# Hybrid decoder step on one core: down-weight differences moved from the attention to the input projection, a third slot for down operands, and another order at the block ends

## The chip, the core and the metric

The kernel runs on one core of a Trainium2 chip. The metric is the time of one execution on the device in microseconds (us). The core has five engines that work side by side and wait for each other by semaphores: PE (matrix products), DVE (vector), ACT (scalar functions and copies), POOL (a second, slower vector engine here) and SP, which in this kernel issues almost all DMA transfers. Each engine executes its instructions strictly in the order in which they were written into its queue.

## The reference, cut to what matters

The function is one step of a decoder layer for a prompt of 2048 positions and a sample group of 32 rows (8 sequences of 4 positions, behind caches of earlier keys and values), followed by a final norm. The model width is 1024, the FFN width 2816.

```python
def _layer_prompt(x, ...):
    q, k, v, u, vg = _project(x, norm1_g, w_in)          # RMSNorm, one product with w_in (1024 x 2560)
    ...
    for (w, d), bias_hj in zip(BRANCHES, biases):        # 8 heads, three dilated windows
        o, l = _dilated_prompt(q, k, v, bias_hj, d, w // d + 1)
    ...
    gate = _spatial_gate(vn, sgu_w, sgu_b).reshape(B, S, D_SGU)
    x = x + jnp.concatenate([att, u * gate], axis=-1) @ w_out
    x = x + _swiglu(x, norm2_g, w_gate, w_up, w_down)
    return x, k[:, S - nw:], v[:, S - nw:]

def _swiglu(x, g, w_gate, w_up, w_down):
    h = _rmsnorm(x, g)
    return (jax.nn.silu(h @ w_gate) * (h @ w_up)) @ w_down
```

The sample rows go through the same layer with the cached keys and values in front of their own, and the window of keys and values is copied into the outputs.

## The kernel before

**Precision.** Everything is fp32, but PE multiplies operands in a shorter format. So each operand is split into a high part (an ACT copy into the short format) and a low part (a subtraction, value less high part, on DVE or POOL), and one product is three matmuls: high by high, high by low, low by high. "Splitting" below always means this pair of operations. In the names, `xh` and `xl`, or the two halves of a `hop` tile, are such parts.

**Stages.** The input projection (0 to 565 us of the span) runs over 240 steps of 24 matmuls each. The order of all that goes on beside them is a list: `Plan.at(step, phase, fn, ...)` files a function under a step and a phase, and `Plan.run` calls them in that order, which writes the instructions into the queues. Beside PE's work lie the sample group's scores and values (`pr`, `kv`, `qv`: cached values loaded by SP; POOL products L539; matmuls L600), and the writing of projected rows to memory. From step B0 = 240 the same list holds the attention (565 to 905 us): for each head and branch `band_scores` (PE, L867 and, for the wide-stride branch, L946) writes scores into the banks `ps_s`, `band_bias` (DVE, L873 and L951) adds the bias and frees the bank, ACT takes exponents, POOL masks and prepares operands (`sq`, `e`), PE turns and multiplies with the values.

**The weights of the down projection.** The FFN is multiplied with a scheme of Strassen's kind: seven products in place of eight, of sums and differences of blocks. The down weights `w_down` are 22 row tiles; a pair n of them (n = 0 to 10), each cut into two column halves of 512, gives the blocks b11, b12 (first row tile) and b21, b22 (second). Seven operands of 128 x 512 per n are kept in memory as `dd_d[n, :, 0..6]`: three plain blocks (copied from memory to memory by `down_plain`, in the projection) and the four differences, made in the attention by `down_rows` (load), `down_sums` (L1231 and L1234: two subtractions on POOL, two on DVE per n) and `down_keep` (store). In the attention they are called at steps 3, 8 to 11 and 11 to 14 of every 14.

**Blocks.** Then the 16 row tiles go in three blocks of 6, 6 and 4, the last one with the sample rows. A block opens with its output projection: `open_unit` (first half of the columns; three matmuls L1414 to L1416 for each of 8 operands, `ps_t`) and `second_unit`, norm (`norm2_*`, L1448 to L1518), then the FFN: for each of 22 hidden tiles f, seven products (`product`, L1799 to L1801), and beside them `h_even` and `h_odd`, which form the operands `hop` of the down products for a pair of hidden tiles, and the down products of the pair before (`down_product`, L1676: 9 matmuls each with 6 tiles). A product index is k = 7n + p. Within the FFN time runs in ticks, one per product; at each, `one(u, q)` calls what is due. Down products stand at SLOT = 2, 4, 6, ... 14 of a pair's 14 ticks.

**Down operands.** `load_dw` (SP) brings operand k into one of the two slots of `B.ring`, `split_dw` splits it (ACT L1655; L1656 on DVE in block 0, on POOL in block 1), `down_product` uses it two ticks after the split is written. Block 1 stores all split operands to `ds_d` (`keep_dw`), and block 2 loads them from there, high and low part, without splitting.

**Block ends.** The last pair's down products (k = K to K + 6 with K = 70) are executed in `next_block`, among the first output units of the following block. There `later(n, fn)` files a function n ticks ahead and `tick()` runs what is due. `h_last` forms the last operands; `split_dw` splits; `finals` are the final norms of the old block's tiles, after each of which the tile's accumulator is stored and loaded with the next block's input rows (`load_acc`); `first_end` adds an output unit's result to it. In the last block the sample rows' unit comes first; its normed rows live in `xns`, in the slot of accumulator 5.

## Time and profile before

| | |
|---|---|
| median of 3 runs | 2578.89 us (2577.04 to 2584.58) |
| profiled execution | 2574.83 us |
| its span | 2573.1 us |
| mean granted PE clock over the span | 0.979 |
| transfers, whole span | 567.45 MB, mean 221 GB/s |

In the views that follow, a row of the windows table gives a stretch of the span, its length, and for each engine the busy time with its number of instructions; then PE's granted clock (1 is full speed), the mean busy share of the 16 DMA engines and what they moved. A row of the waits names the waiting engine, its output and line, what it waited for, and then the total, the number of waits and the longest one in us. A row of the timeline has the start, the duration, engine, line and operation, and in brackets the idle time ahead of it and what ended it. A row by tile or line has the number of instructions and the shortest, median and longest in ns, then the start of the first and the last. A row of the costliest groups has busy time, mean ns of one, and the idle time of the engine ahead of them.

### The profile page before, as it was taken

Reading aid. Unit: us, or ns where it says so; the run is one execution under the profiler, and the core shown is the slowest. Engines: PE = TensorE matmul, PEld = TensorE weight load, DVE = VectorE, ACT = ScalarE, POOL = GpSimd, SP = SyncE. Lnnn points to the kernel's source line nnn. Section 1 sums busy time; section 2 is a strip of 40 time slices with the busy share of each in tenths; the row PEclk is TensorE's granted clock in tenths of the full one; section 3 lists DMA queues with packets and bytes.
Section 4 is the critical chain, followed back from the end, with each engine's and each line's share of the span. In section 5 each row is a group of like instructions: output and inputs, shape, how many; then the busy total and the mean of one; then the engine's idle time right before and its main releaser. Section 6 shows DMA issues by size and latency. Waiting matters only on the chain.

```text
span 2573.1 us, 40785 instructions
## 1 busy us (share of the span) xinstructions
PE 2428.4 (94%) x13764; PEld 2083.0 (81%) x13764; DVE 1683.4 (65%) x3254; ACT 1206.2 (47%) x2703; POOL 1388.9 (54%) x1130
## 2 busy tenths in 40 slices
PE   8999999998989898999999989999999987999997
PEld 6877776667777778899999968988988875988886
DVE  4558572216767645777778777677766766677776
ACT  6324343225656646656666446333433335433334
POOL 2116441004877746777676734655655554666664
PEclk9999999998999899999999999999999998999999
DMA  9975766776668563666667543777777754788884
GB/s 288 282 222 165 240 190 217 224 255 214 236 208 259 161 192 123 212 221 202 223 210 229 187 139 140 235 250 247 244 244 240 242 183 144 266 282 283 285 276 161
DMA packets 360132, 567.45 MB, mean 221 GB/s; under 512 B 36247, under 2 KB 168520, under 8 KB 354804
## 3 DMA queue, kind: packets, MB, share of 16 engines
q1 hardware_dynamic: 353076, 552.78, 66.3%
q10 hardware_dynamic: 6848, 12.06, 1.7%
q8 instruction: 110, 1.80, 0.3%
q14 instruction: 98, 0.80, 0.1%
HBM read 428.77 MB, written 214.73 MB: 250 GB/s over the span
## 4 chain that ended last, share of the span: by engine, by line
PE 36%; POOL 13%; issue 11%; DVE 8%; DMA 7%; ACT 5%; SPq 1%; POOLq 0%; DVEq 0%; ACTq 0%
POOL op L1590 5%; PE ps_o L1676 5%; PE ps_m L1799 4%; PE ps_m L1801 4%; PE ps_m L1800 4%; DMA hop<-dd_d 2%; PE ps_m L1676 2%; PE ps_s L867 1%; POOL sq L938 1%; ACT fr L1558 1%; ACT op L1586 1%; PE ps_o L922 1%; DMA ds_d<-hop 1%; DVE acc L1678 1%; PE ps_s L321 1%
## 5 line engine op out<-in xcount | busy, mean ns | idle before, releaser
L1590 POOL TENSOR_TENSOR op<-fr,op 128x512 fp32r<-128x512 f32 x385 | 505.9, 1330 | 252.4 <-ACT op L1586 240.7
L1799 PE MATMUL ps_m<-xh,op 128*128 128x384 f32 (+3 forms) x1904 | 606.7, 319 | 4.1 <-DVE zn L1820 1.7
L1800 PE MATMUL ps_m<-xl,op 128*128 128x384 f32 (+3 forms) x1904 | 604.4, 317 | 0.8 <-DVE xl L141 0.7
L1801 PE MATMUL ps_m<-xh,op 128*128 128x384 f32 (+3 forms) x1904 | 605.0, 318 | 0.0
L1676 PE MATMUL ps_o<-hop 128*128 128x512 f32 x1272 | 345.9, 401 | 30.6 <-POOL hop L1656 11.8
L1799 PEld LDWEIGHTS ps_m<-xh,op 128*128 128x128 f32 x1904 | 359.9, 189 | 17.8 <-PE ps_m L1801 2.7
L1800 PEld LDWEIGHTS ps_m<-xl,op 128*128 128x128 f32 x1904 | 359.8, 189 | 10.1 <-issue 0.9
L1801 PEld LDWEIGHTS ps_m<-xh,op 128*128 128x128 f32 x1904 | 359.6, 189 | 0.0
L1678 DVE TENSOR_TENSOR acc<-acc,ps_o 128x512 f32<-128x512 f32 x448 | 294.4, 682 | 34.3 <-PE ps_o L1676 30.8
L1676 PEld LDWEIGHTS ps_o<-hop 128*128 128x128 f32 x1272 | 230.0, 188 | 90.1 <-POOL hop L1656 21.7
L1586 ACT ACTIVATE op<-fr 128x512 fp32r<-128x512 f32 x396 | 236.1, 620 | 0.4 <-issue 0.2
L321 PE MATMUL ps_s<-wh,xh 128*128 128x512 f32 x480 | 198.4, 413 | 6.5 <-ACT xh L138 5.9
L322 PE MATMUL ps_s<-wl,xh 128*128 128x512 f32 x480 | 190.1, 396 | 0.0
L323 PE MATMUL ps_s<-wh,xl 128*128 128x512 f32 x480 | 189.9, 396 | 0.0
L1839 ACT ACTIVATE ps_t<-zn 128x384 f32<-128x384 f32 (+1 forms) x126 | 58.3, 463 | 266.7 <-DVE zn L1822 137.1
L1656 POOL TENSOR_TENSOR hop<-hop 128x512 fp32r<-128x512 f32 x71 | 91.8, 1293 | 168.9 <-ACT hop L1655 156.3
L1655 ACT ACTIVATE hop<-hop 128x512 fp32r<-128x512 f32 x142 | 88.8, 625 | 178.5 <-DMA hop<-dd_d 131.3
L539 POOL TENSOR_TENSOR pr<-kv,qb 96x512 f32<-96x512 f32 x32 | 45.7, 1428 | 176.7 <-DMA kv<-in_cache_k_dram 96.0
L321 PEld LDWEIGHTS ps_s<-wh,xh 128*128 128x128 f32 x480 | 91.7, 191 | 49.3 <-issue 23.7
L1590 POOL TENSOR_TENSOR op<-pair,op 128x512 fp32r<-128x512 f32 x63 | 92.6, 1470 | 61.2 <-ACT op L1586 58.1
L1656 DVE TENSOR_TENSOR hop<-hop 128x512 fp32r<-128x512 f32 x71 | 74.3, 1047 | 76.7 <-ACT hop L1655 71.7
L1676 PE MATMUL ps_m<-hop 128*128 128x512 f32 x426 | 122.2, 395 | 0.0
(525 smaller groups left out, 5118.2 us busy)
## 6 DMA issues: line engine op xcount, KB each, us to landing
fr<-ab_d SPq DMA_DIRECT2D x308, 256.0 KB
hop<-dd_d SPq DMA_DIRECT2D x142, 256.0 KB
ds_d<-hop SPq DMA_DIRECT2D x140, 256.0 KB
hop<-ds_d SPq DMA_DIRECT2D x140, 256.0 KB
out_ks_dram<-in_cache_k_dram SPq DMA_DIRECT2D x56, 512.0 KB
out_vs_dram<-in_cache_v_dram SPq DMA_DIRECT2D x56, 512.0 KB
ab_d<-fr SPq DMA_DIRECT2D x88, 256.0 KB
qk_d<-pair SPq DMA_DIRECT2D x64, 256.0 KB
```

Source lines behind the costliest of these rows:

```text
L321: pe.matmul(o[j], xh[:, k, :], wh, start=(k == 0), stop=False)
L322: pe.matmul(o[j], xh[:, k, :], wl, start=False, stop=False)
L323: pe.matmul(o[j], xl[:, k, :], wh, start=False, stop=(k == KD - 1))
L1586: act.activation(ops[f, j][0], ab[f][j], AF.Copy)
L1590: (pool if f or j in POOL_LOW else dve).tensor_sub(lo_, ab[f][j], hi.bitcast(F32))
L1655: act.activation(hi, lo_.bitcast(F32), AF.Copy)
L1656: (pool if B.b0 else dve).tensor_sub(lo_, lo_.bitcast(F32), hi.bitcast(F32))
L1676: pe.matmul(ps, l_, r_, start=(new and y == 0), stop=(y == 2), skip_group_check=True)
L1678: dve.tensor_add(x[:, cs], x[:, cs], ps)
L1799: pe.matmul(out, wh[:, ks], xh[:, :, k], start=(k == 0), stop=False)
L1800: pe.matmul(out, wh[:, ks], xl[:, :, k], start=False, stop=False)
L1801: pe.matmul(out, wl[:, ks], xh[:, :, k], start=False, stop=(k == 3))
```

## The change

Three parts.

1. The four differences of each n are made in the input projection, at steps 124 + 9n to 124 + 9n + 14, all on POOL, each in place in one of seven rotating tiles of 128 x 512 (`tw`): b11 becomes b12 - b11, b12 becomes b22 - b12, then b22 becomes b22 less the new b11, and b21 becomes b21 less that: the same four operands as before, in other places of `dd_d` (PLACE follows). `down_plain` moves out of the projection: three n in the attention, eight in block 0's FFN. SP has 44 loads and 44 stores of 256 KB in place of 22 loads of 512 KB and 44 stores of 256 KB.
2. The ring of down operands has three slots. Operand k + 3 is loaded right behind product k, and split three ticks ahead of its product. Block 2 loads the same unsplit operands as the others and splits them, every third on DVE and the others on POOL; `ds_d`, `keep_dw` and their 280 transfers are gone. In block 2 `h_even` runs on DVE instead of POOL.
3. `next_block` has another order of down products and output units, of the splits, of `h_last` (three parts instead of four), and of the ticks of the halves, finals and ends. The concatenated operands of the first two tiles are loaded in the last ticks of the FFN. Before the last block the finals run in the order 4, 5, 0, 1, 2, 3 instead of 4, 0, 1, 2, 3, 5.

```diff
-    def down_plain(n, j):
-        f, half = 2 * n + (j > 0), int(j == 3)
-        sync.dma_start(dd_d[n, :, j], A["w_down"][f * P:(f + 1) * P, half * 512:(half + 1) * 512])
+    dn = {}
+    def down_rows(n, *js):
+        for j in js:
+            dn[n, j] = w_ = sp.tile([P, 512], F32, name="tw", tag="tw", bufs=7)
+            r0 = (2 * n + j // 2) * P
+            sync.dma_start(w_, A["w_down"][r0:r0 + P, j % 2 * 512:(j % 2 + 1) * 512])
+    def down_sums(n, part):
+        b11, b12, b21, b22 = (dn.get((n, j)) for j in range(4))
+        for x, y, z in (((b11, b12, b11), (b12, b22, b12)), ((b22, b22, b11),), ((b21, b21, b22),))[part]:
+            pool.tensor_sub(x, y, z)
+    def down_keep(n, *js):
+        for j in js:
+            sync.dma_start(dd_d[n, :, 1 + j], dn.pop((n, j)))
+    def down_plain(n):
+        f = 2 * n
+        sync.dma_start(dd_d[n, :, 0], A["w_down"][f * P:(f + 1) * P, 0:512])
+        sync.dma_start(dd_d[n, :, 5:7], A["w_down"][(f + 1) * P:(f + 2) * P, :].rearrange("p (a c) -> p a c", a=2))
...
     for n in range(NF // 2):
-        for y, j in enumerate((0, 2, 3)):
-            at(134 + 6 * n + 2 * y, "store", down_plain, n, j)
+        s0 = 124 + 9 * n
+        at(s0, "misc", down_rows, n, 0, 1, 3)
+        at(s0 + 6, "misc", down_rows, n, 2)
+        for part in range(3):
+            at(s0 + 9 + part, "out", down_sums, n, part)
+        at(s0 + 13, "store", down_keep, n, 0, 1)
+        at(s0 + 14, "store", down_keep, n, 3, 2)
...
-    def down_rows(n):
-        for z in range(2):
-            dn[n, z] = w_ = ap_.tile([P, 2, DA], F32, name="tw", tag="tw", bufs=4)
-            f = 2 * n + z
-            sync.dma_start(w_, A["w_down"][f * P:(f + 1) * P, :].rearrange("p (a c) -> p a c", a=2))
-    def down_sums(n, j, eng):
-        (b11, b12), (b21, b22) = ((dn[n, z][:, 0], dn[n, z][:, 1]) for z in range(2))
-        if j == 1:
-            eng.tensor_sub(b12, b12, b11)
-            return
-        dn[n, "t", j] = t_ = ap_.tile([P, DA], F32, name="tu", tag="tu", bufs=6)
-        eng.tensor_sub(t_, *((b22, b12) if j < 4 else (b21, dn[n, "t", 2])))
-    def down_keep(n, j):
-        if j == 1:
-            sync.dma_start(dd_d[n, :, 1], dn.pop((n, 0))[:, 1])
-        else:
-            sync.dma_start(dd_d[n, :, j + 2], dn.pop((n, "t", j)))
-    for n in range(NF // 2):
-        s0 = B0 + 3 + 14 * n
-        at(s0, "misc", down_rows, n)
-        for j, x, eng in ((3, 5, pool), (1, 6, dve), (2, 7, pool), (4, 8, dve)):
-            at(s0 + x, "store", down_sums, n, j, eng)
-        for j, x in ((3, 8), (1, 9), (2, 10), (4, 11)):
-            at(s0 + x, "store", down_keep, n, j)
+    for n in range(3):
+        at(B0 + 40 + 30 * n, "store", down_plain, n)
...
-        B.ring = [(ts[z][:, 1536:], ts[z + 1][:, 1536:]) for z in (0, 2)]
+        x = fl.tile([P, 512], F32R, name="dwx", tag="dwx", bufs=1)
+        B.ring = [(ts[0][:, 1536:], ts[1][:, 1536:]), (ts[2][:, 1536:], ts[3][:, 768:1280]), (ts[3][:, 1280:1792], x)]
...
     def load_dw(B, k, place=None):
         n, p = divmod(k, 7)
-        B.dw[k] = x = place or B.ring[k % 2]
-        if B.last:
-            for z in range(2):
-                sync.dma_start(x[z].bitcast(F32), ds_d[n, p, z])
-        else:
-            sync.dma_start(x[1].bitcast(F32), dd_d[n, :, PLACE[p]])
+        B.dw[k] = x = place or B.ring[k % 3]
+        sync.dma_start(x[1].bitcast(F32), dd_d[n, :, PLACE[p]])
     def split_dw(B, k):
         hi, lo_ = B.dw[k]
         act.activation(hi, lo_.bitcast(F32), AF.Copy)
-        (pool if B.b0 else dve).tensor_sub(lo_, lo_.bitcast(F32), hi.bitcast(F32))
-    def keep_dw(B, k):
-        n, p = divmod(k, 7)
-        for z in range(2):
-            sync.dma_start(ds_d[n, p, z], B.dw[k][z].bitcast(F32))
+        (dve if B.b0 == 0 or B.last and k % 3 == 0 else pool).tensor_sub(lo_, lo_.bitcast(F32), hi.bitcast(F32))
...
-        eng = pool if B.last or B.b0 == 0 else dve
+        eng = pool if B.b0 == 0 else dve
...
-        B.banks = {i: y for y, i in enumerate(order)}
+        B.banks = {i: (2, 3, 4, 0, 1, 5)[y] for y, i in enumerate(order)}
         B.place()
         tiles = [i for i in order if B.rows[i] == P]
         skip = n - len(tiles)
         for j, i in enumerate(tiles):
-            if j < 3:
-                load_cat(B, i, 0, KD)
-            else:
-                later(2 * j - 5, load_cat, B, i, 0, KD)
-            later((3, 7, 11, 13, 15, 17)[j + skip], split_cat, B, i, dve if j < 2 else pool)
+            if j > 1:
+                later(2 * j - 4, load_cat, B, i, 0, KD)
+            if j:
+                later((0, 1, 5, 8, 10, 12)[j], split_cat, B, i, dve if j % 2 else pool)
...
         for y, fn in enumerate(finals):
-            later(13 + y, fn)
+            later(14 + y, fn)
         for y, i in enumerate(order):
-            later(8 + 2 * n + 2 * y, first_end, B, i)
+            later((19 if B.last else 20) + 2 * y, first_end, B, i)
         for y in range(4):
-            later(13 + 2 * y, half1_split, B, 2 * y, 2 * y + 1)
-            later(15 + 2 * y, sources, B, 0, *((2 * y, 2 * y + 1) if y < 3 else (6,)))
-        K, opens = 7 * (NF // 2 - 1), list(order)
+            later(14 + 2 * y, half1_split, B, 2 * y, 2 * y + 1)
+            later(16 + 2 * y, sources, B, 0, *((2 * y, 2 * y + 1) if y < 3 else (6,)))
+        K = 7 * (NF // 2 - 1)
         def downs(*ks):
             for k in ks:
                 down_product(prev, k)
                 tick()
+        def opens(*ys):
+            for y in ys:
+                open_unit(B, order[y])
+        downs(K - 1)
+        split_dw(prev, K + 1)
         h_last(prev, prev.u, 0)
-        downs(K - 1)
+        downs(K)
+        h_last(prev, prev.u, 1)
         split_dw(prev, K + 2)
-        h_last(prev, prev.u, 1)
-        downs(K + 4)
+        opens(0)
         h_last(prev, prev.u, 2)
         split_dw(prev, K + 3)
-        downs(K)
-        h_last(prev, prev.u, 3)
+        split_dw(prev, K + 4)
+        opens(1)
         split_dw(prev, K + 5)
-        open_unit(B, opens.pop(0))
+        downs(K + 1, K + 2, K + 3)
         split_dw(prev, K + 6)
-        downs(K + 1, K + 2)
-        open_unit(B, opens.pop(0))
-        downs(K + 3, K + 5, K + 6)
-        for i in opens:
-            open_unit(B, i)
+        opens(2)
+        downs(K + 4, K + 5, K + 6)
+        opens(*range(3, n))
         first_operands(B)
...
-                    for y, p in {3: ((0, 0), (1, 1)), 4: ((2, 2), (3, 3)), 5: ((4, 5), (5, 6))}.get(q, ()):
-                        c0 = (y - 4) * 28 * 64 + 512 if y > 3 and nb.last else y * 28 * 64
-                        load_dw(B, 7 * (f // 2) + p, tuple(x[:, c0:c0 + 512] for x in pool_["X"]))
-                    for p in {5: (0,), 6: (4, 1)}.get(q, ()):
-                        split_dw(B, 7 * (f // 2) + p)
+                    for y in {3: (0, 1), 4: (2, 3), 5: (4,)}.get(q, ()):
+                        c0 = 768 if y == 4 and nb.last else y * 28 * 64
+                        load_dw(B, 7 * (f // 2) + 2 + y, tuple(x[:, c0:c0 + 512] for x in pool_["X"]))
+                    if q == 5:
+                        load_cat(nb, 0, 0, KD)
+                        split_dw(B, 7 * (f // 2))
+                    if q == 6:
+                        load_cat(nb, 1, 0, KD)
+                        split_cat(nb, 0, pool)
...
-                    if x == t_ and p == 5 and n + 2 == NF // 2 and nb:
-                        down_product(B, k)
-                        load_dw(B, k + 6, B.ring[k % 2])
-                        continue
                     if n < 0 or n + 1 == NF // 2:
                         continue
-                    if x == t_ - 2 and not B.last:
+                    if x == t_ - 3:
                         split_dw(B, k)
-                    if x == t_ - 1 and nb and nb.last:
-                        keep_dw(B, k)
                     if x == t_:
                         down_product(B, k)
-                    t_ = 14 * ((k - 2) // 7 + 1) + SLOT[(k - 2) % 7] if k > 1 else 9 + k
-                    if x == t_:
+                        if k + 3 < 7 * (NF // 2 - 1) + (2 if nb else 0):
+                            load_dw(B, k + 3)
+                    if k < 3 and x == 8 + k:
                         load_dw(B, k)
+            if bi == 0 and f % 2 == 0 and f < NF - 6 and q == 2:
+                down_plain(f // 2 + 3)
...
-            last = ([4] if nb.last else []) + [i for i in rows if not (nb.last and i == 4)]
+            last = [4, 5, 0, 1, 2, 3] if nb.last else rows
```

How the order changes on the engines, at three places. First DVE in the attention, at the sixth of the eleven n. `ps_s` are score banks, `b` the bias, `e` the biased scores and `st` their sums; `tw` and `tu` are the down weights and their differences. Before:

```order
L905 COPY pt<-ps_o_6974 128x2x128
L873 ISA e,st<-ps_s,b 128x640
L873 ISA st 128x1
L1231 TENSOR_TENSOR tw<-tw 128x512
L905 COPY pt<-ps_t_7009 128x2x128
L873 ISA e,st<-ps_s,b 128x640
L873 ISA st 128x1
L873 ISA e,st<-ps_s,b 128x128
L873 ISA st 128x1
L965 TENSOR_REDUCE st<-e_6960 128x4
L1234 TENSOR_TENSOR tu<-tw,tu 128x512
```

The same place of the changed kernel (L929 is L905 of before, L897 is L873, L989 is L965):

```order
L929 COPY pt<-ps_o_7041 128x2x128
L897 ISA e,st<-ps_s,b 128x640
L897 ISA st 128x1
L929 COPY pt<-ps_t_7074 128x2x128
L897 ISA e,st<-ps_s,b 128x640
L897 ISA st 128x1
L897 ISA e,st<-ps_s,b 128x128
L897 ISA st 128x1
L989 TENSOR_REDUCE st<-e_7027 128x4
```

The two subtractions are gone from between the score operations, and nothing else has moved; the same holds for POOL in the attention.

Second, SP in the projection of the changed kernel, around the end of one n and the start of the next. `raw` are columns of `w_in`, `qv`, `pr` and `kv` cached values of the sample, `qk_d` projected rows on their way to memory.

```order
L633 DMA dd_d<-tw 128x512 x2
L524 DMA qv<-in_cache_v_dram 96x512
L633 DMA dd_d<-tw 128x512 x2
L612 DMA cs_d<-zn 4x512
L623 DMA tw<-in_w_down_dram 128x512
L524 DMA qv<-in_cache_v_dram 96x512
L524 DMA pr<-in_cache_v_dram 96x512
L520 DMA kv<-in_cache_v_dram 96x512
L357 DMA qk_d<-pair 128x4x128 x2
L527 DMA pr<-in_cache_v_dram 128x512
L520 DMA kv<-in_cache_v_dram 96x512
L623 DMA tw<-in_w_down_dram 128x512 x3
```

In the kernel before, the queue there has one copy of a plain block (L619) every two steps and nothing of `tw`. Now the single load (the fourth row tile of the next n) stands directly behind the four stores of this one, and it is the eighth use of the seven tiles.

Third, PE at the end of block 0. L1676 (L1667 after) are the matmuls of down products, with one bank name for each pair of tiles; L1414 to L1416 (L1413 to L1415 after) those of output units. Before, from the last FFN product on:

```order
L1676 MATMUL ps_o_15112<-hop 128x512 x3
L1676 MATMUL ps_o_15117<-hop 128x512 x3
L1676 MATMUL ps_m_15122<-hop 128x512 x3
L1676 MATMUL ps_o_15194<-hop 128x512 x3
L1676 MATMUL ps_o_15199<-hop 128x512 x3
L1676 MATMUL ps_m_15204<-hop 128x512 x3
L1676 MATMUL ps_o_15222<-xh_9302,hop 128x512
L1676 MATMUL ps_o_15222<-xl_9303,hop 128x512
```

Of the changed kernel:

```order
L1667 MATMUL ps_o_15109<-hop 128x512 x3
L1667 MATMUL ps_o_15114<-hop 128x512 x3
L1667 MATMUL ps_m_15119<-hop 128x512 x3
L1667 MATMUL ps_o_15181<-hop 128x512 x3
L1667 MATMUL ps_o_15186<-hop 128x512 x3
L1667 MATMUL ps_m_15191<-hop 128x512 x3
L1413 MATMUL ps_m_15220<-op,xh_9285 128x512
L1414 MATMUL ps_m_15220<-op,xh_9285 128x512
L1415 MATMUL ps_m_15220<-op,xl_9286 128x512
```

The third product, K (K + 4 stood second), is gone from the head, and the first output unit stands there. In all, the order was K - 1, K + 4, K, a unit, K + 1, K + 2, a unit, K + 3, K + 5, K + 6 and the other units; it is K - 1, K, two units, K + 1 to K + 3, a unit, K + 4 to K + 6 and the other units.

More of the change, by code (lines that the diff above doesn't have):

```diff
@@ L122, in hymba_step @@
     dd_d = dram.tile([NF // 2, P, 7, 512], F32, name="dd_d")
-    ds_d = dram.tile([NF // 2, 7, 2, P, 512], F32, name="ds_d")
     ident = consts.tile([P, P], F32, name="ident")
@@ L1454, in norm2_a @@
         else:
-            s1 = fl.tile([P, 4], F32, name="s1", tag="s1", bufs=6)
+            s1 = s1_tile()
             if n != P:
@@ L1765, in h_last @@
             high_of(B, 1, u["s2"], 0, n)
-            for z in (1, 0):
-                high_of(B, 3, a22[z], 0, n, z)
-        elif part == 2:
+        elif part == 1:
             lows_of(B, 1, u["s2"], 0, n)
@@ L2214, in next_block @@
             if front:
-                ahead = (front[0], norm2_t(B, *front, two(ps_m, 0, 1) if (front[0] + B.last) % 2 else None))
+                ahead = (front[0], norm2_t(B, *front, [lambda: ps_m(2), lambda: bank(0)] if front[0] % 2 else two(ps_m, 0, 1)))
             front = i, chain(B, i, ps, ahead)
             if B.last and i == tiles[0]:
-                norm2_c(B, n - 1, B.xns)
+                norm2_c(B, n - 1, B.xns, two(ps_m, 0, 1))
         if B.last:
```

26 lines of the change are left out of this document (13 added, 13 removed).

## The prediction

> **What bounds the kernel now.** First the page's busy times, then the table of windows, cut at the program's stages: the input projection, the attention, and for each token block its opening (last down products, output units, norm) and its FFN. A window's length minus PE's busy time is PE's idle time; PEclk is the granted clock.
>
> ```profile
> PE 2428.4 (94%) x13764; PEld 2083.0 (81%) x13764; DVE 1683.4 (65%) x3254; ACT 1206.2 (47%) x2703; POOL 1388.9 (54%) x1130
> ```
>
> ```profile
> core 0: us, PE busy (x) PEld busy (x) DVE busy (x) ACT busy (x) POOL busy (x), PEclk, DMA share, GB/s
> 300.00:565.00 265.00, 255.78 (x1219) 181.60 (x1220) 98.73 (x191) 82.29 (x136) 51.05 (x38) 0.99 0.69 218
> 565.00:905.00 340.00, 305.12 (x2616) 251.71 (x2614) 230.71 (x549) 207.59 (x528) 237.37 (x241) 0.94 0.68 216
> 905.00:1035.00 130.00, 118.44 (x645) 102.37 (x643) 59.09 (x140) 75.28 (x176) 70.07 (x63) 0.96 0.50 160
> 1035.00:1482.00 447.00, 438.13 (x2263) 404.35 (x2264) 339.89 (x571) 256.71 (x649) 320.89 (x245) 0.99 0.67 213
> 1482.00:1520.00 38.00, 26.99 (x105) 20.12 (x104) 30.18 (x43) 12.48 (x23) 10.43 (x6) 0.91 0.54 157
> 1520.00:1602.00 82.00, 79.41 (x422) 67.93 (x420) 58.79 (x143) 50.41 (x108) 39.75 (x25) 1.00 0.37 126
> 1602.00:2082.00 480.00, 467.69 (x2450) 430.33 (x2449) 338.80 (x558) 185.35 (x384) 289.57 (x222) 1.00 0.75 244
> 2082.00:2110.00 28.00, 21.46 (x91) 15.49 (x90) 18.98 (x31) 9.60 (x19) 17.21 (x13) 1.00 0.62 186
> 2110.00:2197.00 87.00, 70.95 (x336) 57.84 (x335) 53.84 (x136) 47.29 (x103) 34.79 (x23) 0.88 0.37 124
> 2197.00:2520.00 323.00, 318.90 (x2098) 289.81 (x2097) 246.39 (x496) 128.16 (x325) 194.56 (x166) 1.00 0.82 282
> ```
>
> PE is busy 94% of the span, and the change removes no matmul. What it can win is PE's idle time and the time at a lower clock. In the attention (565 to 905) that is 340 - 305.1 = 34.9 us idle, and a clock 6% short over 340 us, some 20 us of work. The two places where one block ends and the next opens idle 11.0 + 2.6 us (1482 to 1602) and 6.5 + 16.1 us (2082 to 2197, clock 0.88). The three FFN stages idle 8.9, 12.3 and 4.1 us. So I read the waits there, the attention's first.
>
> ```profile
> PE ps_s L946 <- DVE st L873: 16.5, 7, 6.3
> PE ps_s L867 <- DVE st L873: 15.1, 13, 4.0
> ...
> POOL tu L1234 <- DMA tw<-in_w_down_dram: 28.1, 2, 23.3
> DVE tw L1231 <- POOL tu L1234: 15.7, 6, 5.1
> ```
>
> 16.5 + 15.1 = 31.6 of the 34.9 us are PE waiting for DVE to free a score bank. DVE itself stood in L1231, a weight difference, for POOL's, 15.7 us; and POOL stood for the down weights' load. The timeline has the chain whole:
>
> ```profile
> 586.33 1.26 POOL L1234 TENSOR_TENSOR tu<-tw 128x512 f32<-128x512 f32 x1 [23.28 <-DMA tw<-in_w_down_dram]
> ...
> 587.62 1.51 DVE L1231 TENSOR_TENSOR tw<-tw 128x512 f32<-128x512 f32 x1 [5.06 <-POOL tu L1234]
> ...
> 590.36 1.94 PE L946 MATMUL ps_s<-sq 128*128 128x128 f32 x8 [6.30 <-DVE st L873]
> 626.44 1.94 PE L946 MATMUL ps_s<-sq 128*128 128x128 f32 x8 [2.45 <-DVE st L873]
> 768.55 1.08 PE L946 MATMUL ps_s<-sq 128*128 128x128 f32 x8 [2.67 <-DVE st L873]
> ```
>
> The load lands, POOL subtracts, DVE's in-place subtraction goes 1.3 us later, and the scores behind it in DVE's queue free PE's bank after 6.30 us. Eight such matmuls take 1.08 us at full clock and 1.94 us behind two of these gaps.
>
> **The change, part by part.** I sum against the profiled execution, 2574.83 us (span 2573.1), which is 4.06 us under the median of the runs, 2578.89.
>
> *1a. The differences leave the attention.* All 44 subtractions go, 22 on POOL and 22 on DVE, with every wait on them. PE's order there is the same, so its tempo tells the worth. One score step (L951) is the beat:
>
> ```profile
> L951 DVE TENSOR_TENSOR e<-ps_s,b x24: 675/680/683, 617.2 to 850.2; 128x512 f32<-128x512 f32 x24
> ...
> L951 DVE TENSOR_TENSOR e<-ps_s,b x9: 676/680/683, 651.0 to 724.5; 128x512 f32<-128x512 f32 x9
> ```
>
> The whole run of 24 has 23 beats in 233.0 us, 10.13 us each. The nine between 651.0 and 724.5, where only small waits fall, have 8 beats in 73.5 us, 9.19 us each. 23 x 0.94 = 21.6 us. Ahead of the first beat lies the 6.30 us gap, and the matmuls behind it lost 0.86 us (1.94 less 1.08), which I double for those that follow: 8 us; behind the last, some 2.5 us more of the same kind (a guess from the smaller gaps). Together **-32**. The bounds: only the 15.7 us of DVE's wait for POOL comes back (-16), or all 31.6 us and half of the 20 us of clock (-42). Next to be late is the softmax chain itself: DVE, ACT and POOL are each busy 61 to 70% here, POOL 28 us less afterwards (22 x 1.26), so none should take over.
>
> [...]
>
> *1b. The differences come into the projection.* 44 POOL subtractions of 1.26 us are 55 us. A step there lasts 565 / 240 = 2.35 us; the work lies at steps 124 to 228, 292 to 537 us, where POOL is busy 51 of 265 us, so there is room. SP gets 44 loads and 44 stores of 256 KB and loses 33 plain copies; the copies lay at 134 to 200, so behind 472 us all of it is new: 2 MB in 9 steps, 98 GB/s on top of a DMA share of 0.69. Behind the new issues in SP's queue stand the weight columns and the sample's cache values:
>
> ```profile
> 446.35 1.06 PE L600 MATMUL ps_t<-pr,z 128*32 128x512 f32 x8 [1.28 <-DMA pr<-in_cache_v_dram]
> ...
> 461.92 0.84 SPq L528 DMA_DIRECT2D pr<-in_cache_v_dram  x1
> ...
> 470.01 0.64 PE L600 MATMUL ps_t<-pr,z 128*32 128x512 f32 x4
> ```
>
> PE meets these values 8.1 us after their issue and has waited 1.28 us for them once. The rotating seven buffers also put a wait into SP: a load for the next n can't be issued before the store of an earlier one has landed. If each of the 11 groups costs one such 1.28 us wait, that is +14. If the copies taken away free something, it can give back the 1.28 us, so -1 is the other end. I take **+4**, nearer to the row's single wait than to eleven.
>
> *2. A third slot for the down operands.* Each is loaded three products ahead and split one product step earlier. What PE waits for now, over the whole run:
>
> ```profile
> PE ps_o L1676 <- POOL hop L1656: 11.8, 17, 1.2
> ...
> PE ps_o L1676 <- ACT hop L1655: 5.8, 12, 2.4
> PE ps_o L1676 <- DVE hop L1656: 5.3, 12, 1.2
> ...
> PE ps_o L1676 <- DMA hop<-ds_d: 2.1, 3, 1.1
> ```
>
> The longest of these, 2.4 us, is less than the product step gained (480 us over 154 products, 3.1 us). In block 1 splits lie on POOL: of its 12.3 us idle the 11.8 us go nearly whole, **-9** (-3 to -12). In block 0 they lie on DVE: **-5** (0 to -8), with eight copies of 768 KB new beside it under a DMA share of 0.67.
>
> *3. Block 2 splits for itself.* The 140 stores in block 1 and 140 loads here go; 70 loads, 70 ACT copies and 70 subtractions come, 24 on DVE and 46 on POOL, and three DVE operations a pair replace POOL's. The prices:
>
> ```profile
> L1656 POOL TENSOR_TENSOR hop<-hop 128x512 fp32r<-128x512 f32 x71 | 91.8, 1293 | 168.9 <-ACT hop L1655 156.3
> L1655 ACT ACTIVATE hop<-hop 128x512 fp32r<-128x512 f32 x142 | 88.8, 625 | 178.5 <-DMA hop<-dd_d 131.3
> ...
> L1656 DVE TENSOR_TENSOR hop<-hop 128x512 fp32r<-128x512 f32 x71 | 74.3, 1047 | 76.7 <-ACT hop L1655 71.7
> ...
> 2414.56 1.29 POOL L1590 TENSOR_TENSOR op<-fr,op 128x512 fp32r<-128x512 f32 x1 [1.95 <-ACT op L1586]
> ...
> 2414.61 1.52 DVE L1698 TENSOR_TENSOR hop<-zn,hop 128x256 fp32r<-128x256 f32 x1
> 2417.59 0.41 DVE L1698 TENSOR_TENSOR hop<-zn,hop 128x256 fp32r<-128x256 f32 x1
> ```
>
> A pair takes about 33 us here (323 us, nearly ten pairs), DVE 25 of them. It gains 2.4 x 1.05 us of splits and three operations of 0.41 to 1.52 us, 3.8 to 7.1 us, so it ends at 87 to 97% busy. ACT's 70 x 0.625 = 44 us lie in its 195 us idle, POOL's 46 x 1.29 = 59 us in its 128 us. PE waits for DVE's operands only where they cluster. At 0.7 us for each split on DVE that falls there (24 x 0.7 = 17, half of it covered), less the 2.1 us for ds_d, I take **+7**; -3 if all is covered, +20 if none is and every halved operation meets a POOL operation as at 2414.6.
>
> *4. The block ends.* Before, three down products stand at the head, then an output unit, and the rest; now two products, then two output units, under which the splits run. The transition to block 1 idles 13.6 us, to block 2 22.6 us, and the largest gaps of the second are
>
> ```profile
> 2135.95 0.67 DVE L1429 TENSOR_TENSOR acc<-acc,ps_t 32x512 f32<-32x512 f32 x1 [2.68 <-DMA acc<-in_x_sample_dram]
> ...
> 2140.36 0.69 PE L1419 MATMUL ps_o<-wol,cats 128*64 128x512 f32 x1 [4.77 <-ACT wol L138]
> ...
> 2152.96 1.05 ACT L1459 ACTIVATE xns<-acc 32x1024 f32<-32x1024 f32 x1 [7.74 <-DMA out_yp_dram<-acc]
> ...
> 2157.32 1.06 PE L1480 MATMUL ps_t<-ident,xns 32*128 32x32 f32 x8 [5.26 <-ACT xns L1467]
> ```
>
> The sample row's square waits until the slot acc5 is stored; its tile now ends second instead of last, so the 5.26 us gap should go. The chain behind the last down product (final norm, store, reload of acc, then first ends) is the same and PE has less output work left to lay over it. So half of the idle time: **-6** of 13.6 (-11 to +2), **-8** of 22.6 plus 10 us of clock (-15 to +3).
>
> **Sum:** 4 - 32 - 5 - 6 - 9 - 8 + 7 = -49; 2574.8 - 49 = 2525.8, plus 4.1 for the median: **2530**. Bounds taken together as roots of squares: 28 us up, 19 down.
>
> **Rivals.** (a) *The attention keeps a bound of its own*: with the subtractions gone, the softmax chain (POOL 70% busy) is late by as much, and only -16 comes: 2546. For it: a third of the beats are quiet already; against: the quiet beats hold 9.19 us with subtractions among them. (b) *The reorder wins nothing*, the reload chain eats it, so that it doesn't do what it is written for: +14, 2544. (c) *DVE fills up in block 2*: each added operation meets a POOL operation as at 2414.61, 1.1 us longer, so that a pair's 5.4 added ones cost 9 us, DVE passes its 33 us, and block 2 costs +20: 2543. For it: that row; against: DVE's rows at 0.41 us beside it. [...] (d) *SP stalls in the projection*, the slower side: at each group the load stands for the store, with weight columns and values behind it. If PE loses the whole 8.1 us trip in 10 groups, +81 for +4: 2607. From 5.3 us a group on ((49 + 4) / 10) it cancels all the rest; the single wait of 1.28 us and an idle POOL, which makes stores prompt, speak against.
>
> **Numbers.** Forecast 0.61 (its own range 2511 to 2541); (a) 0.12, (b) 0.07, (c) 0.09, all faster; (d) 0.05; two or more of the first three with smaller misses together, within 0.3% of before (7.7 us, about what a measurement of this kernel can tell from no change), 0.06. Range 2508 to 2560. Faster 0.89, same 0.06, slower 0.05.
>
> **What would show it.** In the profile after: PE's idle time between 565 and 905 falls from 34.9 us to 5 to 10 and the clock to 0.98 or more; L951's beats stand at 9.2 us; waits on POOL's splits nearly vanish; the xns gap is gone; block 2's window grows by under 20 us. I am wrong if the projection ends more than 15 us later, or if L867 and L946 go on waiting for DVE with nothing of the weights in its queue.

## The result and the profile after

| | before | changed |
|---|---|---|
| median | 2579.32 us (4 runs, 2577.04 to 2584.58) | 2535.37 us (4 runs, 2531.66 to 2541.51) |
| ratio | | 0.9829, 95% interval 0.9804 to 0.9854 |
| profiled execution, span | 2574.83, 2573.1 us | 2534.40, 2532.6 us |

The kernel is 1.7% faster; 2530 was forecast. To set the stages side by side I cut both traces at the same events on PE: the last matmul of the projection, the first output unit, and the first and last FFN product of each block. Here are the windows of the changed kernel between these events: projection, attention, FFN of block 0, block end, FFN of block 1, block end, FFN of block 2.

```profile
core 0: us, PE busy (x) PEld busy (x) DVE busy (x) ACT busy (x) POOL busy (x), PEclk, DMA share, GB/s
0.00:579.20 579.20, 552.62 (x2556) 416.86 (x2556) 279.20 (x512) 209.49 (x344) 206.72 (x153) 0.98 0.80 253
579.20:872.30 293.10, 284.59 (x2588) 234.00 (x2586) 206.17 (x527) 203.93 (x527) 203.98 (x220) 0.99 0.56 174
961.70:1457.70 496.00, 478.45 (x2564) 444.80 (x2561) 362.92 (x618) 284.70 (x722) 358.98 (x277) 1.00 0.70 218
1457.70:1555.30 97.60, 88.46 (x401) 71.25 (x400) 76.62 (x165) 54.63 (x114) 37.96 (x25) 1.00 0.48 155
1555.30:2029.40 474.10, 473.59 (x2562) 446.18 (x2563) 348.16 (x578) 189.48 (x396) 296.83 (x227) 1.00 0.54 172
2029.40:2132.70 103.30, 81.07 (x337) 62.06 (x335) 67.95 (x151) 50.13 (x108) 40.21 (x28) 0.87 0.40 128
2132.70:2504.20 371.50, 357.30 (x2343) 325.71 (x2342) 306.21 (x600) 180.75 (x427) 264.43 (x199) 0.99 0.66 214
```

Two windows of the kernel before, cut at the same events: the attention and the FFN of block 1.

```profile
571.00:904.70 333.70, 298.82 (x2588) 246.46 (x2587) 230.41 (x549) 207.29 (x527) 237.07 (x241) 0.94 0.68 216
1587.20:2083.10 495.90, 481.91 (x2565) 444.12 (x2562) 349.08 (x587) 194.50 (x402) 297.29 (x228) 1.00 0.73 236
```

The length of each stage, with the forecast of its change beside what came:

| stage | before | changed | change | forecast |
|---|---|---|---|---|
| input projection | 571.0 | 579.2 | +8.2 | +4 |
| attention | 333.7 | 293.1 | -40.6 | -32 |
| opening of block 0 | 86.9 | 89.4 | +2.5 | 0 |
| FFN of block 0 | 493.2 | 496.0 | +2.8 | -5 |
| end of block 0 | 102.4 | 97.6 | -4.8 | -6 |
| FFN of block 1 | 495.9 | 474.1 | -21.8 | -9 |
| end of block 1 | 101.5 | 103.3 | +1.8 | -8 |
| FFN of block 2 | 360.0 | 371.5 | +11.5 | +7 |
| tail | 28.4 | 28.4 | 0 | 0 |
| span | 2573.1 | 2532.6 | -40.5 | -49 |

So the total hides misses that cancel: the attention and block 1 gave 21 us more than forecast, six other stages 30 us less. The waits of PE over the whole run say where the new ones are (their largest rows, L1667 and L1786 being the down products and FFN products of the changed kernel):

```profile
PE ps_o L1667 <- DVE acc L1669: 19.4, 19, 2.6
PE ps_m L1786 <- DVE raw L1807: 11.1, 9, 1.3
PE ps_t L599 <- DMA pr<-in_cache_v_dram: 6.2, 4, 3.4
...
PE ps_m L1479 <- ACT xns L1466: 5.8, 1, 5.8
...
PE ps_s L891 <- DVE st L897: 2.5, 6, 0.4
```

PE's waits for split operands are nearly gone, and its waits for a score bank fell from 15.1 to 2.5 us at L867 (now L891) and from 16.5 to 0.7 us at L946 (now L970). In their place PE waits for DVE to free banks of down products (mostly in block 2), for DVE's `raw` (block 0), for cached values (projection), and for `xns` as before.

### The profile page after: what moved, and what is told of

The parts are those of the page before. It is cut to its first block, busy times and chain, and to the rows that moved or that the text cites. A ratio compares the mean times of both kernels' runs of the same rounds, so it can differ in the third digit from the quotient of the medians.

```text
span 2532.6 us, 40744 instructions
## 1 busy us (share of the span) xinstructions
PE 2410.7 (95%) x13764; PEld 2075.1 (82%) x13764; DVE 1705.0 (67%) x3289; ACT 1236.6 (49%) x2773; POOL 1457.5 (58%) x1165
## 4 chain that ended last, share of the span: by engine, by line
PE 54%; DVE 14%; DMA 9%; ACT 8%; issue 7%; POOL 7%; SPq 1%; ACTq 0%; DVEq 0%; POOLq 0%
PE ps_o L1667 7%; PE ps_m L1786 7%; PE ps_m L1788 6%; PE ps_m L1787 6%; PE ps_m L1667 2%; PE ps_s L891 2%; PE ps_o L946 2%; PE ps_s L320 2%; DVE hop L1689 2%; PE ps_s L321 2%; ACT fr L1557 2%; PE ps_s L322 2%; ACT op L1585 2%; DVE acc L1669 2%; POOL op L1589 2%
## 5 line engine op out<-in xcount | busy, mean ns | idle before, releaser
L1589 POOL TENSOR_TENSOR op<-fr,op 128x512 fp32r<-128x512 f32 x385 | 518.8, 1362 | 194.2 <-ACT op L1585 147.0
L1786 PE MATMUL ps_m<-xh,op 128*128 128x384 f32 (+3 forms) x1904 | 608.5, 320 | 17.3 <-DVE raw L1807 11.1
L1786 PEld LDWEIGHTS ps_m<-xh,op 128*128 128x128 f32 x1904 | 360.7, 189 | 34.6 <-issue 15.4
L1787 PEld LDWEIGHTS ps_m<-xl,op 128*128 128x128 f32 x1904 | 360.7, 189 | 9.3 <-DVE xl L1502 0.4
L1667 PE MATMUL ps_o<-hop 128*128 128x512 f32 x1142 | 325.0, 396 | 18.0 <-DVE acc L1669 17.1
L1667 PEld LDWEIGHTS ps_o<-hop 128*128 128x128 f32 x1142 | 209.5, 188 | 59.6 <-ACT ps_t L1826 13.9
L1652 DVE TENSOR_TENSOR hop<-hop 128x512 fp32r<-128x512 f32 x72 | 87.0, 1208 | 88.2 <-ACT hop L1651 88.1
L1589 POOL TENSOR_TENSOR op<-pair,op 128x512 fp32r<-128x512 f32 x63 | 82.3, 1307 | 75.9 <-ACT op L1585 72.2
L629 POOL TENSOR_TENSOR tw<-tw 128x512 f32<-128x512 f32 x44 | 60.3, 1370 | 113.3 <-DMA tw<-in_w_down_dram 86.8
L1667 PE MATMUL ps_m<-hop 128*128 128x512 f32 x384 | 119.4, 392 | 0.0
```

The costliest lines, as they stand in the source:

```text
L629: pool.tensor_sub(x, y, z)
L1589: (pool if f or j in POOL_LOW else dve).tensor_sub(lo_, ab[f][j], hi.bitcast(F32))
L1652: (dve if B.b0 == 0 or B.last and k % 3 == 0 else pool).tensor_sub(lo_, lo_.bitcast(F32), hi.bitcast(F32))
L1667: pe.matmul(ps, l_, r_, start=(new and y == 0), stop=(y == 2), skip_group_check=True)
L1786: pe.matmul(out, wh[:, ks], xh[:, :, k], start=(k == 0), stop=False)
L1787: pe.matmul(out, wh[:, ks], xl[:, :, k], start=False, stop=False)
```

## The experiments

Every kernel ran on the chip beside the kernel before; stage lengths are from one profiled execution of each, cut at the same events.

**The parts apart.** One kernel has part 1 alone; the other has all but part 1. Both are put together from the two versions' own lines, so that no new code is in them. The core of it, as part 1 alone changes the kernel before (the other kernel has it the other way round):

```diff
-            at(134 + 6 * n + 2 * y, "store", down_plain, n, j)
+        s0 = 124 + 9 * n
+        at(s0, "misc", down_rows, n, 0, 1, 3)
...
-        for j, x, eng in ((3, 5, pool), (1, 6, dve), (2, 7, pool), (4, 8, dve)):
-            at(s0 + x, "store", down_sums, n, j, eng)
...
+        at(B0 + 40 + 30 * n, "store", down_plain, n)
...
-    PLACE = (0, 4, 5, 6, 2, 1, 3)
+    PLACE = (0, 4, 2, 3, 5, 1, 6)
```

> The kernel before with part 1 alone (differences made in the projection, plain copies in attention and block 0). Theory (the parts act each in its own stage and add up): projection 571.0 -> about 579 us, attention 333.7 -> about 293, the FFN stages as before (493, 496, 360 within 3 us); 2579 - 32 = about 2547. Rival (the attention's gain needs the lighter traffic of the other parts too, or the copies in block 0 cost there): attention stays above 305, or block 0's FFN grows by 5 us or more; 2558 or above.

> The changed kernel with part 1 undone (differences in the attention as before, plain copies in the projection; third slot, block 2's splits and block ends as changed). Theory (the parts add): the attention goes back to about 334 us with PE waiting some 30 us for DVE, everything else stays; the projection, 574 to 583 us in eight profiles with part 1 and 571 in the one without, comes to 574 or less; total 2535 + 41 - 7 = about 2569. Rival (the projection's length has nothing to do with part 1 and only spreads from run to run): it comes to 575 us or more, total about 2576.

Part 1 alone: 2547.4 us, ratio 0.9878 (0.9847 to 0.9909); projection 579.5, attention 292.8, FFN stages 496.0, 494.1, 360.1. All but part 1: 2570.93 us, ratio 0.9984 (0.9968 to 1.0001); projection 570.6, attention 334.8. The first part carries most of the gain. Parts 2 and 3 without it are worth some 4 us, hardly to be told from nothing; beside it they bring the median from 2547.4 to 2535.37 us, 12 us, with intervals that overlap a little. Stage by stage the parts act apart: the attention is long or short with part 1, block 1 and block 2 with the others (474.1 and 375.0 us without part 1). Two windows of the kernel without part 1 have the old projection and attention back:

```profile
0.00:570.60 570.60, 550.50 (x2556) 416.12 (x2556) 276.26 (x512) 209.59 (x345) 150.26 (x109) 0.99 0.74 231
570.60:905.40 334.80, 297.87 (x2588) 243.98 (x2586) 228.45 (x549) 207.00 (x527) 236.69 (x241) 0.95 0.67 215
```

As to the projection: ten profiles with part 1 at its place gave 574.3 to 582.5 us, two without it 571.0 and 570.6. The cost is real, and it spreads by some 8 us from one execution to the next. Only in block 0's FFN they don't add: it was 493.2 us before, and is 496.0 with part 1 alone, 496.2 without part 1 (so without copies there) and 496.0 with all parts. With part 1 alone PE waits there 11.3 us for split operands, 8.8 before; with the other parts it waits 11 us for `raw` in their place.

**The block ends as before** (part 3 undone, from the lines of the kernel before; its core):

```diff
-        downs(K)
+        downs(K + 4)
...
-        opens(0)
+        downs(K)
...
-        opens(1)
+        open_unit(B, opens.pop(0))
...
-            last = [4, 5, 0, 1, 2, 3] if nb.last else rows
+            last = ([4] if nb.last else []) + [i for i in rows if not (nb.last and i == 4)]
```

> The changed kernel with the block ends in the order of before (part 3 undone). Theory (the reorder won 4.7 us at the first block end and lost 2.4 at the second): the stretches between the last FFN product of a block and the first of the next go from 98.0 and 104.2 back to about 103 and 102 us, FFN of block 1 stays at 474; 2535 + 2 = about 2538. Rival (block 1's clean pace hangs on the block end's new order): FFN of block 1 goes above 480, total 2550 or more.

2534.22 us (ratio 0.9832, 0.9805 to 0.986), against 2535.37: the reorder as a whole moves nothing that can be measured. The two block ends are 102.2 and 100.6 us, against 97.6 and 103.3 with it: it wins some 4.6 us at the first and loses 2.7 at the second. Block 1's FFN stays at 474.1, so its clean pace doesn't hang on the order.

**What made block 1 faster.** Three kernels. The first only splits later:

```diff
-                    if x == t_ - 3:
+                    if x == t_ - (3 if B.last else 2):
                         split_dw(B, k)
```

> The changed kernel with splits two ticks ahead of their product in blocks 0 and 1 instead of three (three slots, loads and block 2 as changed). Theory (the tick gained is what took away the waits in block 1, and in block 0 it only moved the wait from the split operand to DVE's L1807): FFN of block 1 from 473.7 to about 490 us with PE waiting for POOL's hop again; block 0 from 495.6 to about 492, its waits for raw L1807 (11.1 us) gone and those for hop back; total 2535 + 13 = about 2548. Rival (the 140 stores that are gone made block 1 faster): its FFN stays within 476, total about 2532 to 2536.

2536.23 us, block 1's FFN 474.3, block 0's 497.0. The theory fell: block 1 is as clean with the split two ticks ahead. That left the earlier load and the stores that are gone, and the next two take one each. The second kernel loads and splits with the timing of two slots; the third puts the 140 stores back:

```diff
-                        if k + 3 < 7 * (NF // 2 - 1) + (2 if nb else 0):
-                            load_dw(B, k + 3)
+                        if k + 2 < 7 * (NF // 2 - 1):
+                            load_dw(B, k + 2)
...
+                    if x == t_ - 1 and nb and nb.last:
+                        keep_dw(B, k)
                     if x == t_:
                         down_product(B, k)
```

> The changed kernel with the timing of two slots: operand k + 2 is loaded behind product k, and split two ticks ahead (all blocks); no stores in block 1. Since splitting two ticks ahead alone left block 1 at 474.3 us, either the earlier load or the missing stores made it clean. Theory A (the load: before, ACT's split waited for it, 131 us of idle time put down to hop<-dd_d): block 1's FFN from 474 to 488 us or more, POOL's hop waited for again. Theory B (the 140 stores): block 1 stays within 476.

> The changed kernel with the 140 stores of split operands put back into block 1 (nothing reads them), three slots and splits three ticks ahead. Theory A (the earlier load made block 1 clean): block 1's FFN stays within 478 us, total 2535 to 2539. Theory B (the stores were what made operands late): 488 us or more, total 2548 or more.

With loads late and no stores block 1's FFN is 474.2; with loads early and stores it is 486.6 (two executions each; medians 2544.38, where block 2 took 384.9, and 2556.8). The first is as theory B had it; the second is 1.4 us short of B's 488 and 8.6 us over A's 478. So the stores are the cause, and the earlier load takes part of their cost away. The rows that had it are SP's own waits in block 1 (engine SP, first of the kernel before, from 1587 to 2083 us, then of the changed kernel with the stores):

```profile
SPq L1651 <- DMA ds_d<-hop: 224.8, 69, 5.5
```

```profile
SPq L1648 <- DMA ds_d<-hop: 145.1, 46, 5.5
SPq L1648 <- DMA ds_d<-dwx: 75.9, 23, 5.5
```

A load into a slot has to wait until the slot's last content is stored, not only until PE has used it. SP stood for these stores for 225 us, up to 5.5 us each, with the FFN's own loads queued behind it; the operand came late to ACT, and so to POOL and PE. With three slots SP stands for the stores as long, 221 us, and the lateness reaches PE by another way. These are waits of ACT, DVE and PE in block 1 of the kernel with the stores:

```profile
ACT hop L1652 <- DMA dwx<-dd_d: 29.4, 12, 4.1
ACT hop L1652 <- DMA hop<-dd_d: 26.6, 14, 4.4
```

```profile
DVE hop L1695 <- ACT hop L1699: 64.4, 23, 7.9
```

```profile
PE ps_o L1673 <- DVE acc L1675: 9.8, 5, 2.9
```

ACT stands for the operand, with the high part of a hidden tile (L1699) behind it in its queue; DVE stands for that one, 64.4 us against 28.9 in the changed kernel, with the accumulation that frees PE's bank behind; no wait of PE for a split operand is left among its rows.

Four cases make the table: stores and late loads 495.9 (before; 494.1 with part 1 alone), stores and early loads 486.6, no stores and late loads 474.2, no stores and early loads 474.1. Loading and splitting earlier covers 8 or 9 of the 20 to 22 us while the stores are there and nothing once they are gone. In block 2 it does matter: 384.9 with loads and splits late, 371.5 as changed.

**The second block end.** In the changed kernel `xns` no longer waits for its slot (ACT L1458, 1.45 us, against 7.74 before), and yet PE waits 5.85 us for it. The rows of SP, DVE, ACT and PE that lead there, in order of time:

```profile
2080.65 10.06 SPq L1544 DMA_DIRECT2D fr<-ab_d  x4
2090.80 0.38 SPq L1905 DMA_DIRECT2D out_yp_dram<-acc  x1
2091.28 0.38 SPq L1339 DMA_DIRECT2D acc<-in_x_prompt_dram  x1
...
2097.43 0.69 DVE L1424 TENSOR_TENSOR acc<-acc,ps_m 128x512 f32<-128x512 f32 x1 [4.28 <-DMA acc<-in_x_prompt_dram]
...
2103.09 1.15 ACT L1466 ACTIVATE xns<-acc,h 32x1024 f32<-32x1024 f32 x1 [0.47 <-DVE h L148]
...
2104.29 1.05 PE L1479 MATMUL ps_m<-ident,xns 32*128 32x32 f32 x8 [5.85 <-ACT xns L1466]
```

Four loads of FFN operands (`fr`) take SP 10.06 us, as they wait for their tiles; behind them stand the store and the reload of the first tile's accumulator; DVE waits 4.28 us for that in `first_end`, and the sample row's factor `h` is queued behind it on DVE. The experiment calls these loads three ticks later:

```diff
-            later(16 + 2 * y, sources, B, 0, *((2 * y, 2 * y + 1) if y < 3 else (6,)))
+            later((19 if B.last else 16) + 2 * y, sources, B, 0, *((2 * y, 2 * y + 1) if y < 3 else (6,)))
```

> The changed kernel with the FFN's first operands (the fr loads) called three ticks later at the last block end, so that SP does not stand 10.06 us in them ahead of the accumulator's store and reload. Theory (the slot's wait of 7.7 us is gone, and the sample row's norm is late because DVE waits 4.28 us for tile 0's reload, which stands behind those loads in SP's queue): the xns wait of 5.8 us falls below 2.5, the stretch 104.2 falls to about 100; 2535 - 4 = about 2531. Rival (the chain of final norms sets it in any case): the stretch stays at 103 or more.

2527.27 us, ratio 0.9806 (0.9776 to 0.9835). The block end is 97.7 us, and the wait for `xns` isn't among PE's waits there any more; 5.6 of the 8 us come from this stage; the projection was 4.9 us shorter this time and block 2's FFN 2.4 longer, which is spread.

**Blocks 2 and 0.** Two kernels change a place in each. In block 2, all splits on POOL, or `h_even` back on POOL; in block 0, the split four ticks ahead, or three ahead but written at the head of the tick:

```diff
-        (dve if B.b0 == 0 or B.last and k % 3 == 0 else pool).tensor_sub(lo_, lo_.bitcast(F32), hi.bitcast(F32))
+        (dve if B.b0 == 0 else pool).tensor_sub(lo_, lo_.bitcast(F32), hi.bitcast(F32))
...
-                    if x == t_ - 3:
+                    if x == t_ - (4 if B.b0 == 0 else 3):
```

> Two stages apart. Block 2: all 70 splits on POOL. Theory (DVE, with 24 splits of 1.36 us and 25 us of waiting for ACT's half of them in its queue, is late to free PE's banks): block 2's FFN from 371 to about 362 us, waits for acc nearly gone. Rival (the three operations of h_even on DVE do it): it stays above 368. Block 0: splits four ticks ahead, so on other ticks than DVE's L1807. Theory: block 0's FFN from 496 to about 484, the eleven us of waits for raw gone. Rival (ACT's scaling of the gate operands, 2.44 us a piece, holds the split back wherever it stands): 493 to 497.

```diff
-        eng = pool if B.b0 == 0 else dve
+        eng = pool if B.last or B.b0 == 0 else dve
...
+            if bi == 0 and u["b"] == B.nt:
+                for k in range(7 * (NF // 2 - 1)):
+                    if 7 * u["f"] + q == 14 * (k // 7 + 1) + SLOT[k % 7] - 3:
+                        split_dw(B, k)
             product(B, u, q)
```

> Two stages apart. Block 2: h_even back on POOL, splits as changed (every third on DVE). Theory (DVE's splits are what is late): block 2's FFN stays above 367 us. Rival (h_even): about 362. Block 0: splits three ticks ahead as changed, but written at the head of the tick, ahead of ACT's scaling of the gate operands. Theory (ACT's queue makes DVE's half of the split late, and that DVE's L1807): waits for raw gone, block 0's FFN about 484. Rival (DVE is late by itself): 493 to 497.

The first: 2518.76 us (ratio 0.9773, 0.9754 to 0.9792), block 2's FFN 362.6, block 0's 494.1 with 10.6 us of waits for `raw`. The second: 2533.63 us (0.9838, 0.9815 to 0.9861), block 2's 371.9, block 0's 497.4. So block 2's loss is DVE's splits; `h_even` back on POOL gives nothing while they are there. The rows of the changed kernel in block 2, the tile's (count, then ns) and DVE's waits:

```profile
L1652 DVE TENSOR_TENSOR hop<-hop x24: 675/1364/1683, 2158.9 to 2500.2; 128x512 fp32r<-128x512 f32 x24
```

```profile
DVE hop L1652 <- ACT hop L1651: 25.4, 19, 2.0
```

24 splits of 1.36 us, and 25.4 us in which DVE stands for ACT's half of them with the accumulations that free PE's banks behind. The lengths bear this out: the seven kernels with these splits, loaded as in the changed one, took 371.5 to 375.0 us in block 2, the three without them 360.7 to 362.6. The way from the splits to PE is shown only in part. With them gone PE still waits 11.2 us for `acc` there, 13.4 with them, which is not the "nearly gone" that was expected; 6.4 of the 8.9 us are PE's busy time.

In block 0 both theories on the tick fell. What the trace has there, on ACT, DVE and PE:

```profile
1064.52 2.44 ACT L1557 ACTIVATE fr<-fr,g2c 128x128 f32<-128x128 f32 x8
1066.86 0.62 ACT L1651 ACTIVATE hop<-hop 128x512 fp32r<-128x512 f32 x1
...
1067.51 0.69 DVE L1652 TENSOR_TENSOR hop<-hop 128x512 fp32r<-128x512 f32 x1 [2.24 <-ACT hop L1651]
1068.11 0.55 DVE L1806 TENSOR_TENSOR raw<-raw,ps_m 128x384 f32<-128x384 f32 x1
1068.70 0.56 DVE L1807 TENSOR_TENSOR raw<-raw,ps_m 128x384 f32<-128x384 f32 x1
1069.40 0.41 PE L1786 MATMUL ps_m<-xh,op 128*128 128x384 f32 x1 [1.25 <-DVE raw L1807]
```

ACT scales eight pieces (2.44 us), then copies the high part; DVE has stood 2.24 us for it, and L1806 and L1807, which free a bank of PE, are behind. Of two successive hidden tiles one has a split at that place whichever tick is taken. If DVE's standing is the cause, another engine has to take the subtraction:

```diff
-        (dve if B.b0 == 0 or B.last and k % 3 == 0 else pool).tensor_sub(lo_, lo_.bitcast(F32), hi.bitcast(F32))
+        pool.tensor_sub(lo_, lo_.bitcast(F32), hi.bitcast(F32))
```

> The changed kernel with the FFN's first operands three ticks later at the last block end, as in t2_src, and every split's subtraction on POOL, in block 0 too. The two earlier runs' gains should add: second block end 98 us and block 2's FFN 362 us, 8 + 9 us; of block 0 the theory is that DVE is late at L1807 because the subtraction ahead of it stands 2.24 us for ACT's half, so with it on POOL the eleven us of waits for raw go and its FFN is about 484 us: total 2535 - 8 - 9 - 12 = about 2506. Rival (POOL, busy 72% in block 0, or ACT, is then late with the FFN's operands): block 0's FFN stays at 493 or more, total about 2518.

2499.9 us, ratio 0.9682 (0.9661 to 0.9702), with block 0's FFN at 483.2, block 1's end at 95.6 and block 2's FFN at 360.7. (One of its five timed executions took 6007.26 us, the others 2494 to 2502; why is open, and the ratio leaves it out.) POOL is busier by 72 us in block 0 and DVE less by 34, and PE's waits there are now:

```profile
PE ps_o L1667 <- POOL hop L1652: 2.8, 5, 1.4
PE ps_m L1786 <- DVE raw L1815: 1.4, 1, 1.4
```

This version beats both kernels by far: what the changed kernel wins over the one before, 1.7%, becomes 3.2%.

**The projection.** The last kernel has the order of the second block end and the POOL splits of block 2, and makes the differences 44 steps earlier:

```diff
-        s0 = 124 + 9 * n
+        s0 = 80 + 9 * n
```

> The changed kernel with t2_src's order, block 2's splits all on POOL (block 0 as changed), and the differences of the projection 44 steps earlier (from step 80 on), where DMA is busy 66 to 75% instead of 83 to 87%. Theory (the loads and stores of the differences make the sample's cached values late, 6.2 us of waits for pr after 400 us, and the clock lost behind them): those waits fall to 2 us or less, the projection's length, 574 to 583 us in six profiles, comes to 572 or less; total about 2513. Rival (POOL's subtractions beside the gate's operands, or the run's own spread, set the projection): it stays in 574 to 583 us, total about 2518.

2521.43 us; the projection is 583.5 us. The waits for `pr` are gone from PE's largest, and others stand there (S_s 4.0 us, zn 3.8 us). The theory fell: the waits moved, and the cost stayed. Which of the loads, stores and subtractions makes it was not taken apart.

## Why the prediction came out right

The total is nearer than its parts deserve: 2535.37 for 2530, while the terms miss by 21 us to one side and 30 to the other. That is luck. Part 1 was forecast at -28 and gave -32 by itself; parts 2 and 3 were forecast at -21 and gave some -4 by themselves, -12 beside part 1.

- **1a, the attention: right in its cause, mis-sized.** -40.6 for -32. DVE's order without the two subtractions gave PE most of what it had waited for: 34.9 us idle (333.7 less 298.8 busy) became 8.5. DVE had stood for POOL not only the 15.7 us at L1231, on which I put my lower bound, but 10.5 more at L1234, and each of PE's gaps over 1.2 us there came right behind one of these two lines. (The down weights' loads and stores left the stage with the subtractions, and no run takes one without the other; but no wait of PE there was for a DMA.) The other 14.2 us are PE's busy time, 298.8 to 284.6 for the same 2588 matmuls, as the clock went from 0.94 to 0.99; I had given the clock about half of its 20 us at most. The clock was at half speed in seven stretches of this stage, 37.5 us in all, and in one of 3.4 us afterwards. The row at 768.55, of which I said that the eight matmuls ran at full clock behind a gap of 2.67 us, has such a stretch too; it began just behind the eight. These windows lie ahead of two of the stretches and in them:

```profile
622.99:626.40 3.41, 1.00 (x9) 0.74 (x7) 3.31 (x8) 1.98 (x7) 1.42 (x2) 1.00 0.02 3
626.41:633.23 6.82, 6.79 (x43) 6.11 (x45) 3.96 (x9) 2.69 (x6) 2.19 (x3) 0.50 0.53 167
766.37:769.77 3.40, 1.22 (x11) 1.25 (x12) 3.40 (x6) 1.04 (x3) 3.32 (x4) 1.00 0.40 154
769.90:773.10 3.20, 3.20 (x22) 2.84 (x22) 2.31 (x7) 1.79 (x4) 0.67 (x2) 0.50 0.00 0
```

  The beats stand at

```profile
L975 DVE TENSOR_TENSOR e<-ps_s,b x24: 678/680/682, 616.9 to 821.9; 128x512 f32<-128x512 f32 x24
```

  that is 205.0 / 23 = 8.91 us, for the same 24 beats that took 10.13 (they are the fifth to the 28th of 32, not all, as I put it). The quiet stretch that I took for the floor, 9.19, still held subtractions. In the trace of before, half clock came with gaps of 2.35, 2.45 and 2.67 us of this stage, from 848.27, 626.41 and 769.77 us on.
- **1b, the projection: right in sign and bound, +8.2 for +4.** PE's waits for cached values went from 1.3 us in one to 6.2 us in four, and the clock from 0.99 to 0.98. What makes it stays open, as the last experiment says. Rival (d), SP standing for the stores, didn't come: SP's waits for the differences' stores are not among its large ones.
- **2, the third slot: block 1 right in sign, wrong in cause, and over twice the size.** -21.8 came for -9. I laid the gain of 9 us to an operand loaded and split earlier. The runs show that it came from the stores which I had listed under step 3 without a price. Their cost was to be read in SP's waits, which I didn't look at for block 1. The size is off for a second reason: a wait cost more than its gap. At one of 0.85 us the rows before have these starts:

```profile
1650.38 0.49 PE L1676 MATMUL ps_o<-hop 128*128 128x512 f32 x1
1651.73 1.43 PE L1676 MATMUL ps_o<-hop 128*128 128x512 f32 x5 [0.85 <-POOL hop L1656]
1653.68 0.33 PE L1799 MATMUL ps_m<-xh,op 128*128 128x384 f32 x1
...
1659.94 0.33 PE L1799 MATMUL ps_m<-xh,op 128*128 128x384 f32 x1
```

  The two FFN products and the down product with the wait last 7.67 us (from 1646.01), the next three, without, 6.26: 1.41 us lost for 0.85 shown. The matmul ahead of the gap is recorded with 0.49 us, while in a stream the next one follows after 0.23, so the gap shows 0.26 us too little; the matmuls on either side start 0.29 us late in all. Over block 1's FFN, idle time fell by 13 us and PE's busy time by 8, to 68 such stretches of 6.27 us in a row.
- **2, block 0: wrong.** -5 was forecast, +2.8 came. The step that failed is "the longest of these, 2.4 us, is less than the product step gained": the split's two halves lie on queues, and DVE's half, written a tick earlier, stood in front of L1807 for ACT. A wait took the place of the one removed: 8.8 us for split operands before, 11.1 us for `raw` after.
- **3, block 2: right in sign, +11.5 for +7,** inside its bounds. The cost was where I put it, DVE's 24 splits, but not for rival (c)'s reason in whole: all splits on POOL give back 8.9 us while `h_even` gives none. The splits do last 1.36 us, twice the 0.68 of the fastest. Of the 24, 20 began while POOL was in a subtraction of its own (L1589) and ended 0.55 us after it; three of the four fast ones began 0.28 us into one, and that one then took 2.1 us in place of 1.3. The 25.4 us of waiting for ACT come on top.
- **4, the block ends: -4.8 for -6 right, +1.8 for -8 wrong.** The slot's wait went as I said; what I missed is what was late next: the accumulator's reload, behind loads in SP's queue that stand for their tiles. Rival (b) is nearly what happened over both ends together, -3.0 us for -14.

## What to carry to other kernels

In this kernel an in-order queue passed a wait on to what stood behind it (at the second block end SP's 10.06 us became 4.28 us of DVE's and 5.85 us of PE's): before moving an operation, read what it will wait for at its new place and what is queued behind it, on SP's queue as well as on the engines. Here a subtraction that needs another engine's half belonged on the engine whose queue frees no bank of PE (block 0's FFN took 496.0 us with it on DVE, 483.2 on POOL). When a change has several parts, size each from the waits of its own stage, SP's too, since a right total can hide parts that are wrong by 10 us each way.

## What was unexpected of the hardware

PE's idle time in the trace was less than what a stall cost: 0.85 us of gap went with 1.41 us of a longer tick, because recorded matmuls of a stream overlap (0.33 us long, 0.17 us apart). And waits of 2 to 6 us in the attention cost a second sum, 14.2 us of PE's busy time for unchanged matmuls, as the granted clock rose from 0.94 to 0.99 when they went.

Such a mean hides two values: in the traces of before and of the changed kernel the granted clock is recorded as 1 or 0.5, with nothing between. The half-clock stretches, 20 before and 17 in the changed kernel, last 3.41, 6.83, 10.24 or 13.65 us (the last of each trace, 9.89 and 9.55 us, is cut off by its end), and within a trace they begin whole multiples of 3.41 us apart. In the attention before, two waits of nearly one length differed in their place among these steps. A gap of 2.35 us (845.15 to 847.50) lay within one: PE was busy for 1.06 us of 844.86 to 848.27, and the next 3.41 us were at half clock. One of 2.29 us (816.93 to 819.22) lay across two, with PE busy for 2.79 and 1.75 us of them, and the clock stayed at 1 to 824.38 and beyond. What decides such cases isn't shown.
